# Routed experts in two halves: the down product in three float32r passes, run amid the next expert's gate and up products

## The chip, the cores and the metric

The kernel runs on one core of one Trainium2 chip. The metric is the device time of one execution in microseconds; the time of a version is the median of its runs.

## The reference, cut to what matters

Two transformer layers run one after the other on 512 tokens of width 1024. The first one ends in a mixture of 64 experts, of which each token takes 8, plus one shared expert. Only the routed experts are touched here:

```python
def swiglu(x, wg, wu, wd):
    return (jax.nn.silu(x @ wg) * (x @ wu)) @ wd
...
    def expert_block(acc, blk):
        tok, wt, e = blk
        yb = swiglu(h_pad[tok], w_e_gate[e], w_e_up[e], w_e_down[e]) * wt[:, None]
        return acc.at[tok].add(yb), None
...
    return swiglu(h, w_sh_gate, w_sh_up, w_sh_down) + routed[:n]
...
    return x + g_ffn * y.reshape(b, s, d)
```

`wg` and `wu` are 1024 x 256, `wd` is 256 x 1024, all float32. A block holds up to 128 tokens of one expert; with 512 tokens, 8 experts each and 64 experts, a block has 64 real tokens on the average and the rest of its 128 places is padding. `wt` is a token's weight for the expert and `g_ffn` a vector of 1024 gains.

## The kernel before

The stages follow one another: the first layer's mixing part (`block1`), the experts (`moe`), the second layer's mixing part (`mixer`) and its key-value lookup (`peer`). The experts take the stretch from about 620 to 1375 us of the profiled execution.

`moe` (line 764) loops over the 64 experts. Each has three weight loads of 1 MB on the SP queue (`expert_load`, line 1020; parts 0 and 1 hold gate and up, part 2 holds down) into nine rotating buffers called `raw`, and a gather of its token rows from `h2d` on the POOL queue (`next_rows`, line 1034) into one of three buffers `xg`. A 65th block (`spare`, line 1088, called at e = 32) takes tokens past the 128th of one expert; `overflow` (line 1092) is a loop for still more of them.

`expert_block` (line 1039) does one block:

- eight transposes of `xg` on TensorE and a split of the result into a high and a low float32r part `xt` (`split`, line 104: ScalarE copies to the high part, VectorE subtracts for the low part).
- gate and up product into one PSUM tile `p_gu`: the weights are split in four pieces of 128 x 1024 into pairs `whi`, `wlo` (three buffers of each, pool `pair`), and each piece feeds two chunks of three passes (`mm`, line 91: high by high, high by low, low by high). That makes 24 matmuls of 512 columns.
- `ea` = silu(gate) on ScalarE, times up on VectorE (lines 1060 and 1061), two transposes into `p_at`, a VectorE copy to `eat` (line 1066).
- the down product in plain float32 straight from the `raw` buffer (line 1072): two column halves by two chunks, four matmuls, which the profile shows as eight records.
- VectorE multiplies each half by the token weight and by `grow`, which holds g_ffn in every row (line 1075), and an indirect DMA on the POOL queue adds the 128 rows to one of two DRAM sums `yd` (line 1076). The padding places carry the row numbers 512 to 639, for which `yd` has 128 spare rows; the gather of line 1031 has the bound 511 and leaves out what lies past it.

Consecutive experts use the two sums in turn; experts 62 and 63 both add to `yd[1]`. While expert 63 runs, `routed_first` (line 1135) loads `yd[0]`, and `routed_second` (line 1144) adds it to the residual rows `xr`; `routed` (line 1200) does the same with `yd[1]` after the stage, and from there everything depends on it.

The order on each engine comes from the framework, which plays a timeline through as it builds and lets ready work go ahead (`schedule_with_timeline_sim=True`); instructions of the experts before and after are thus already mixed on TensorE. VectorE's order is the written one in the block of expert 63, and VectorE, ScalarE and SP follow the written order in `routed`.

Between the experts stands other work: `slots` every eighth (line 908, indices for the next eight experts, VectorE above all), `ffn_input` at e = 11, the shared expert in float32 (`shared`, `shared_down`) at eight of the experts, `by_tokens` at two.

## Time and profile before

| what | us |
|---|---|
| median of 3 runs | 3178.13 (3173.89 to 3178.19) |
| the profiled execution | 3173.92 |
| its span | 3172.1 |
| TensorE busy in the span | 3062.8 |
| VectorE / ScalarE / GpSimd busy | 2238.7 / 1383.4 / 578.9 |

The span is the time from the first to the last instruction of the profiled execution; 1.8 us of its own time lie around it. A matmul's duration runs from its start to its modelled end; since matmuls are pipelined, what one costs in a row of them is the distance between two starts. PE is TensorE's matmul row, PEld its weight loads, DVE VectorE, ACT ScalarE, POOL GpSimd, SP the engine that issues most DMAs.

### The profile page before, as it was taken

How to read it: one execution, taken by the hardware profiler on the slowest of the kernel's cores; microseconds unless marked ns; L12 is line 12 of the kernel's file. 1: busy time of each engine (PE TensorE's matmuls, PEld its weight loads, DVE VectorE, ACT ScalarE, POOL GpSimd, SP SyncE). 2: the span in 40 equal slices, each digit the busy share in tenths (PEclk: the TensorE clock that was granted, in tenths of full speed). 3: DMA queues.
4: the chain of work that ended last, by engine and by line, in shares of the span. 5: the costliest groups of instructions: out<-in, count | busy, mean ns of one | idle time of the engine just before them, and what ended most of it. 6: DMA issues, size and time to landing. Idle time of an engine off the chain costs nothing.

```text
span 3172.1 us, 43671 instructions
## 1 busy us (share of the span) xinstructions
PE 3062.8 (97%) x16232; PEld 2479.5 (78%) x16232; DVE 2238.7 (71%) x4079; ACT 1383.4 (44%) x2199; POOL 578.9 (18%) x448
## 2 busy tenths in 40 slices
PE   8999999999999999969999999999999999999999
PEld 4777888666666766657777788899999998888887
DVE  7467654587777777756633334899998887888887
ACT  5257423454444544434445324544444443333332
POOL 0200000122222222200000000033333233222221
PEclk9999999899999999989999999999999999999999
DMA  7554545399999999952121122487789989999997
GB/s 248 175 159 145 220 158 203 125 359 338 335 344 334 358 349 346 317 170 83 41 85 62 70 93 95 139 283 268 278 312 348 332 332 344 349 348 354 353 339 270
DMA packets 237626, 782.01 MB, mean 247 GB/s; under 512 B 28884, under 2 KB 110292, under 8 KB 191588
## 3 DMA queue, kind: packets, MB, share of 16 engines
q1 hardware_dynamic: 169072, 574.02, 49.0%
q0 software_dynamic: 65424, 198.81, 20.2%
q10 hardware_dynamic: 2916, 6.37, 0.6%
q8 instruction: 128, 2.10, 0.3%
q14 instruction: 86, 0.70, 0.1%
HBM read 694.38 MB, written 101.97 MB: 251 GB/s over the span
## 4 chain that ended last, share of the span: by engine, by line
PE 49%; DVE 6%; issue 1%; ACT 1%; DMA 1%; ACTq 0%; DVEq 0%; POOL 0%; POOLq 0%
PE p_y L102 16%; PE p_pu L102 12%; PE p_za L102 3%; PE p_z L102 2%; PE p_all L1267 2%; PE p_rg L102 1%; DVE wlo L106 1%; PE p_pq L102 1%; PE p_mx L102 1%; PE p_yr L102 1%; DVE prow L2010 1%; PE r_s L1614 1%; PE r_y L1624 1%; PE p_ya L102 1%; PE p_gt L1979 1%
## 5 line engine op out<-in xcount | busy, mean ns | idle before, releaser
L105 ACT ACTIVATE whi<-raw 128x1024 fp32r<-128x1024 f32 (+1 forms) x686 | 711.5, 1049 | 1135.4 <-PE p_pu L102 259.7
L106 DVE TENSOR_TENSOR wlo<-raw,whi 128x1024 fp32r<-128x1024 f32 (+1 forms) x686 | 822.6, 1207 | 350.2 <-ACT whi L105 338.9
L102 PE MATMUL p_pu<-xp,whi 128*128 128x384 f32 x2048 | 531.3, 338 | 5.0 <-ACT pact L1845 4.8
L102 PEld LDWEIGHTS p_pu<-xp,whi 128*128 128x128 f32 x2048 | 369.2, 188 | 7.9 <-ACT pact L1845 7.6
L102 PE MATMUL p_gu<-whi,xt 128*128 128x512 f32 x1040 | 356.8, 411 | 0.2 <-ACT whi L105 0.2
L102 PE MATMUL p_pu<-xp,wlo 128*128 128x384 f32 x1024 | 344.8, 338 | 4.7 <-DVE wlo L106 4.7
L102 PE MATMUL p_y<-whi,vhi 128*128 128x512 f32 x768 | 299.1, 389 | 3.0 <-ACT vhi L2060 1.6
L102 PE MATMUL p_y<-wlo,vhi 128*128 128x512 f32 x768 | 298.9, 389 | 0.0
L2000 POOL DMA_INDIRECT prow<-in_pu_rows,rows x128 | 198.0, 1547 | 513.9 <-DVE prow L2010 365.6
L1072 PE MATMUL p_y<-raw,eat 128*128 128x512 f32 x520 | 237.1, 597 | 2.7 <-DVE eat L1066 1.5
L102 PE MATMUL p_y<-whi,vlo 128*128 128x512 f32 x768 | 237.8, 389 | 0.0
L102 PEld LDWEIGHTS p_gu<-whi,xt 128*128 128x128 f32 x1040 | 197.4, 190 | 50.4 <-issue 11.2
L102 PE MATMUL p_gu<-wlo,xt 128*128 128x512 f32 x520 | 223.0, 429 | 4.9 <-DVE wlo L106 4.7
L2000 POOL DMA_INDIRECT prow<-in_pv_rows,rows x128 | 139.5, 1090 | 363.0 <-DVE yr L2016 349.7
L102 PEld LDWEIGHTS p_pu<-xp,wlo 128*128 128x128 f32 x1024 | 192.3, 188 | 10.4 <-DVE wlo L106 10.2
L1072 PEld LDWEIGHTS p_y<-raw,eat 128*128 128x128 f32 x520 | 97.7, 191 | 101.6 <-issue 89.5
L102 PEld LDWEIGHTS p_y<-whi,vhi 128*128 128x128 f32 x768 | 144.1, 188 | 33.5 <-ACT vhi L2060 2.0
L1076 POOL DMA_INDIRECT yd<-ey,gidx x64 | 117.5, 1836 | 285.1 <-DVE ey L1075 268.1
L102 PEld LDWEIGHTS p_y<-wlo,vhi 128*128 128x128 f32 x768 | 144.2, 188 | 30.0
L102 PEld LDWEIGHTS p_y<-whi,vlo 128*128 128x128 f32 x768 | 144.2, 188 | 29.9
L2016 DVE SCALAR_TENSOR_TENSOR yr<-prow,pdots,yr 128x1024 f32<-128x1024 f32 x128 | 163.8, 1280 | 0.2
L2010 DVE SCALAR_TENSOR_TENSOR prow<-prow,xr 128x1024 f32<-128x1024 f32 x128 | 155.5, 1219 | 3.1 <-DMA prow<-in_pu_rows,rows 3.0
(703 smaller groups left out, 5558.7 us busy)
## 6 DMA issues: line engine op xcount, KB each, us to landing
raw<-in_w_moe SPq DMA_DIRECT2D x195, 1024.0 KB
raw<-in_pu SPq DMA_DIRECT2D x64, 1024.0 KB
raw<-in_pv_rows SPq DMA_DIRECT2D x64, 1024.0 KB
raw<-in_w_mod SPq DMA_DIRECT2D x24, 1024.0 KB
gd<-gst SPq DMA_DIRECT2D x12, 2048.0 KB
vgt<-gd SPq DMA_DIRECT2D x32, 768.0 KB
actd<-pact SPq DMA_DIRECT2D x54, 384.0 KB
vact<-actd SPq DMA_DIRECT2D x54, 384.0 KB
```

Source lines behind the costliest of these rows:

```text
L102: nc.tensor.matmul(out, a, b, start=start and i == 0, stop=stop and i == len(passes) - 1)
L105: self.nc.scalar.activation(hi, src, AF.Copy)
L106: (lo_engine or self.nc.vector).tensor_tensor(lo, src, hi.bitcast(F32), ALU.subtract)
L1072: nc.tensor.matmul(py, at[:, 128 * k:128 * k + 128], wd[:, 1024 * k + 512 * n:1024 * k + 512 * n + 512], start=k == 0, stop=k == 1)
L1076: nc.gpsimd.indirect_dma_start(out=yd[:], out_offset=bass.IndirectOffsetOnAxis(ap=gi, axis=0), in_=y[:], in_offset=None, bounds_check=639, ...
L1267: self.nc.tensor.matmul(pts[i][:, :264], w[a][:, 128 * k:128 * k + 128], self.hn[b][:, k, 264 * i:264 * i + 264], start=k == 0 and n == 0, ...
L1614: nc.tensor.matmul(pt[:m, :n], self.rk[r:r + 64, g, 128 * kt:128 * kt + m], self.rq[r:r + 64, g, 512 - n:], start=True, stop=True)
L1624: nc.tensor.matmul(o, sts[kt][:, 128 * (i - kt):128 * (i - kt) + 128], v[:, 128 * kt:128 * kt + 128], start=False, stop=kt == i)
L1979: nc.tensor.matmul(pt[:, i, :], hots["hot2"][:, g, :, t], hots["ghi"][:, g, :, t], start=True, stop=False)
L2000: nc.gpsimd.indirect_dma_start(out=t[:], out_offset=None, in_=A["pu_rows" if i < 128 else "pv_rows"], in_offset=bass.IndirectOffsetOnAxis( ...
L2010: nc.vector.scalar_tensor_tensor(t, t, 1.0, self.xr, ALU.mult, ALU.mult, accum_out=dots[:, k:k + 1])
L2016: nc.vector.scalar_tensor_tensor(self.yr, t, dots[:, k:k + 1], self.yr, ALU.mult, ALU.add)
```

## The change

Five things are done. `expert_block` is cut into `expert_in` (transposes and split of the rows), `expert_up` (gate, up, and the product `ea`) and `expert_down` (the rest), and the loop runs the down half of expert e - 1 and the input half of expert e + 1 between the four pieces of expert e's gate and up product. The down product takes three float32r passes on split weights, two pieces more per expert through the `pair` buffers. The token weight goes into the product `ea`; VectorE's two evictions of the down product become ScalarE copies, and g_ffn is multiplied on the sums, in `routed_second` and `routed`. The scatter has the bound 511 and leaves out the padding places, so `yd` has 512 rows. `grow` lives in another pool.

```diff
-            self.yd = [d.tile([640, 1024], F32, name=f"yd{i}") for i in range(2)]
+            self.yd = [d.tile([512, 1024], F32, name=f"yd{i}") for i in range(2)]
...
+            down, xt = iter(()), self.expert_in(xg.pop(0))
+
+            def beside(down, e):
+
+                nonlocal xt
+                next(down, None)
+                yield
+                if e < 64:
+                    xt = self.expert_in(xg.pop(e))
+                yield
+                yield from down
+
             for e in range(64):
...
                     w[e] = self.expert_load(e)
-                    xg[e] = self.next_rows(self.gidx[:, e:e + 1])
+                if 2 <= e + 1 < 64:
+                    xg[e + 1] = self.next_rows(self.gidx[:, e + 1:e + 2])
...
-                    self.expert_block(xg.pop(e), self.gidx[:, e:e + 1], self.wsl[:, e:e + 1], w.pop(e), yd)
+                    other = beside(down, e + 1)
+                    up = self.expert_up(xt, self.wsl[:, e:e + 1], w.pop(e), other)
+                    for step in other:
+                        pass
+                    down = self.expert_down(*up, self.gidx[:, e:e + 1], yd)
                     if e == 63:
+                        for step in down:
+                            pass
                         self.routed_second()
...
                     self.mm(pg, (xt[0][:, k, :], xt[1][:, k, :]), (hi[:, 512 * kk:512 * kk + 512], lo[:, 512 * kk:512 * kk + 512]),
                             k == 0, k == 7)
+                next(other, None)
         a = ms.tile([128, 256], F32, name="ea", tag="ea")
         nc.scalar.activation(a, pg[:, :256], AF.Silu)
-        nc.vector.tensor_mul(a, a, pg[:, 256:])
+        nc.vector.scalar_tensor_tensor(a, a, ws, pg[:, 256:], ALU.mult, ALU.mult)
+        return a, part
+
+    def expert_down(self, a, part, gi, yd):
...
-        at = ms.tile([128, 256], F32, name="eat", tag="eat")
-        nc.vector.tensor_copy(at, pt[:, :256])
+        at = [ms.tile([128, 256], F32R, name=f"eat{i}", tag=f"eat{i}") for i in range(2)]
+        self.split(*at, pt[:, :256])
+        yield
         y = ms.tile([128, 1024], F32, name="ey", tag="ey")
         wd = part(2)
+        py = [ps.tile([128, 512], F32, name="p_y", tag="y") for n in range(2)]
+        for k in range(2):
+            hi, lo = (self.pair.tile([128, 1024], F32R, name=n, tag=n) for n in ("whi", "wlo"))
+            self.split(hi, lo, wd[:, 1024 * k:1024 * k + 1024])
+            for n in range(2):
+                self.mm(py[n], tuple(t[:, 128 * k:128 * k + 128] for t in at), (hi[:, 512 * n:512 * n + 512], lo[:, 512 * n:512 * n + 512]),
+                        k == 0, k == 1)
         for n in range(2):
-            py = ps.tile([128, 512], F32, name="p_y", tag="y")
-            for k in range(2):
-                nc.tensor.matmul(py, at[:, 128 * k:128 * k + 128], wd[:, 1024 * k + 512 * n:1024 * k + 512 * n + 512],
-                                 start=k == 0, stop=k == 1)
-            o = slice(512 * n, 512 * n + 512)
-            nc.vector.scalar_tensor_tensor(y[:, o], py, ws, self.grow[:, o], ALU.mult, ALU.mult)
+            nc.scalar.activation(y[:, 512 * n:512 * n + 512], py[n], AF.Copy)
         nc.gpsimd.indirect_dma_start(out=yd[:], out_offset=bass.IndirectOffsetOnAxis(ap=gi, axis=0),
-                                     in_=y[:], in_offset=None, bounds_check=639, oob_is_err=True, compute_op=ALU.add)
+                                     in_=y[:], in_offset=None, bounds_check=511, oob_is_err=False, compute_op=ALU.add)
...
     def routed_second(self):
         for x, y in zip(self.xr, self.y0):
+            self.nc.vector.tensor_mul(y, y, self.grow[:, None, :].to_broadcast([128, 2, 1024]))
             self.nc.vector.tensor_add(x, x, y)
...
         for t in range(4):
+            nc.vector.tensor_mul(ys[t], ys[t], self.grow)
             nc.vector.tensor_add(x[t], x[t], ys[t])
```

## Rows read from the trace of the kernel before

**Rows 1.** The page's busy time and share of the span, TensorE.
```profile
PE 3062.8 (97%) x16232; PEld 2479.5 (78%) x16232; DVE 2238.7 (71%) x4079; ACT 1383.4 (44%) x2199; POOL 578.9 (18%) x448
```

**Rows 2.** Windows: stretch, length, busy per engine (instructions), clock, DMA share, GB/s.
```profile
620.00:1358.00 738.00, 726.35 (x3110) 493.14 (x3107) 556.29 (x815) 358.28 (x479) 200.69 (x127) 0.99 0.97 335
...
740.00:780.00 40.00, 37.08 (x139) 23.64 (x137) 25.99 (x41) 19.55 (x28) 7.75 (x6) 0.91 0.87 305
```

**Rows 3.** Waits in 620 to 1358: total us, times, longest.
```profile
PE p_gu L102 <- DVE wlo L106: 4.7, 5, 1.6
...
DVE wlo L106 <- ACT whi L105: 90.2, 64, 7.1
...
ACT whi L105 <- PE p_gu L102: 239.4, 116, 10.2
```

**Rows 4.** DMA in 620 to 1358: queues (packets, MB, share), issues by line.
```profile
q1 hardware_dynamic: 27827, 197.42, 67.0%
q0 software_dynamic: 18144, 49.52, 29.9%
...
yd<-ey,gidx POOLq DMA_INDIRECT x63
xg<-h2d,gidx POOLq DMA_INDIRECT x62
```

**Rows 5.** Timeline of TensorE: start, us, one down product, then gate and up passes.
```profile
856.96 3.60 PE L1072 MATMUL p_y<-raw,eat 128*128 128x512 f32 x8
...
1328.21 0.39 PE L102 MATMUL p_gu<-wlo,xt 128*128 128x512 f32 x1
...
1330.30 0.40 PE L102 MATMUL p_gu<-wlo,xt 128*128 128x512 f32 x1
```

**Rows 6.** Groups of instructions in 620 to 1358: busy us, mean ns, idle before.
```profile
L106 DVE TENSOR_TENSOR wlo<-raw,whi 128x1024 fp32r<-128x1024 f32 x257 | 309.1, 1221 | 91.4 <-ACT whi L105 90.2
L105 ACT ACTIVATE whi<-raw 128x1024 fp32r<-128x1024 f32 x257 | 266.2, 1064 | 246.9 <-PE p_gu L102 239.4 <-PE p_at L1064 4.1 <-DVE ea L1061 0.9
L1072 PE MATMUL p_y<-raw,eat 128*128 128x512 f32 x520 | 237.1, 597 | 2.7 <-DVE eat L1066 1.5 <-DVE ey L1075 1.2
...
L1075 DVE SCALAR_TENSOR_TENSOR ey<-p_y,wsl,grow 128x512 f32<-128x512 f32 x128 | 91.3, 745 | 15.5 <-PE p_y L1072 15.2
L106 DVE TENSOR_TENSOR xt<-p_xt,xt 128x512 fp32r<-128x512 f32 x130 | 84.8, 684 | 15.8 <-ACT xt L105 15.7
...
L105 ACT ACTIVATE xt<-p_xt 128x512 fp32r<-128x512 f32 x130 | 71.7, 595 | 74.9 <-PE p_gu L102 65.8 <-PE p_xt L1046 7.6
...
L1066 DVE COPY eat<-p_at 128x256 f32<-128x256 f32 x65 | 27.4, 422 | 24.7 <-PE p_at L1064 24.0
L1061 DVE TENSOR_TENSOR ea<-ea,p_gu 128x256 f32<-128x256 f32 x65 | 26.8, 413 | 9.8 <-ACT ea L1060 9.8
L1060 ACT ACTIVATE ea<-p_gu 128x256 f32<-128x256 f32 x65 | 25.3, 390 | 26.2 <-PE p_gu L102 26.2
```

**Rows 7.** A window of the last layer in which VectorE is nearly full; columns as in Rows 2.
```profile
2220.00:2300.00 80.00, 75.59 (x422) 72.43 (x421) 78.61 (x291) 34.27 (x49) 29.83 (x18) 1.00 0.77 278
```

**Rows 8.** Timeline of the stage's end: start, us, engine, line.
```profile
1354.00 1.54 POOL L1076 DMA_INDIRECT yd<-ey,gidx  x1 [3.70 <-DVE ey L1075]
...
1357.85 0.75 DVE L1075 SCALAR_TENSOR_TENSOR ey<-p_y,wsl,grow 128x512 f32<-128x512 f32 x1 [0.96 <-PE p_y L1072]
...
1363.76 3.18 POOL L1076 DMA_INDIRECT yd<-ey,gidx  x1 [8.22 <-issue]
```

**Rows 9.** The chain that ended last, in order of time: start, us, what.
```profile
1363.76 10.65 DMA yd<-ey,gidx
```

**Rows 10.** Groups of VectorE instructions in 1358 to 1392; columns as in Rows 6.
```profile
L1217 DVE TENSOR_TENSOR h2f<-h2f,yx 128x1024 f32<-128x1024 f32 x4 | 4.9, 1217 | 0.0
L1146 DVE TENSOR_TENSOR h2f<-h2f,raw 128x2048 f32<-128x2048 f32 x2 | 4.6, 2286 | 4.6 <-DMA raw<-yd 4.6
```

More of the change, by code (lines that the diff above doesn't have):

```diff
@@ L347, in qkv @@
                         for y in self.yd:
-                            for i in range(5):
+                            for i in range(4):
                                 nc.gpsimd.dma_start(y[128 * i:128 * i + 128, :], self.macc)
@@ L716, in ffn_begin @@
         self.r4 = r.tile([128, 4], F32, name="r4")
+        self.grow = r.tile([128, 1024], F32, name="grow")
         r = self.pool(self.rs, "h2r", side="right")
@@ L771, in moe @@
             self.sact = q.tile([128, 2, 512], F32, name="sact")
-            self.grow = q.tile([128, 1024], F32, name="grow")
             self.xr = [t.rearrange("p a b -> p (a b)").rearrange("p (t d) -> p t d", d=1024) for t in self.h2f]
@@ L1039, in expert_block, with expert_in @@
     def expert_block(self, xg, gi, ws, w, yd):
+        for step in self.expert_down(*self.expert_up(self.expert_in(xg), ws, w), gi, yd):
+            pass
+    def expert_in(self, xg):
         nc, ps, ms = self.nc, self.mp, self.ms
@@ L1047, in expert_block, with expert_up @@
             self.split(*(t[:, 4 * g:4 * g + 4, :].rearrange("p a b -> p (a b)") for t in xt), pt)
+        return xt
+    def expert_up(self, xt, ws, w, other=iter(())):
+        nc, ps, ms = self.nc, self.mp, self.ms
         pg = ps.tile([128, 512], F32, name="p_gu", tag="mm")
@@ L1058, in expert_block @@
                             k == 0, k == 7)
+                next(other, None)
         a = ms.tile([128, 256], F32, name="ea", tag="ea")
         nc.scalar.activation(a, pg[:, :256], AF.Silu)
-        nc.vector.tensor_mul(a, a, pg[:, 256:])
+        nc.vector.scalar_tensor_tensor(a, a, ws, pg[:, 256:], ALU.mult, ALU.mult)
+        return a, part
+    def expert_down(self, a, part, gi, yd):
+        nc, ps, ms = self.nc, self.mp, self.ms
         pt = ps.tile([128, 512], F32, name="p_at", tag="tb")
```

## The prediction

> **What bounds the kernel now.** TensorE is busy in 97% of the span [rows 1], so I went to the windows of the one stage that the change touches, 620 to 1358 us: TensorE is busy in 726.35 of 738 us, VectorE in 556.29, ScalarE in 358.28, and the DMA engines in 97% of it [rows 2]. Two resources look full, and a reader has to decide which one sets the pace. The waits tell: what ScalarE waits for before it splits a weight piece is TensorE, 239.4 us in 116 times, because the `whi` buffers are still in use; VectorE waits 90.2 us for ScalarE; TensorE's matmuls wait for VectorE only 4.7 us [rows 3]. Nobody waits for a load worth speaking of. So TensorE sets the pace, its order being dense already, and every microsecond of its matmuls in this stage is a microsecond of the kernel. The DMA engines just keep up. That matters for the change: a stage that gets shorter with the same traffic would run into them.
>
> What fills them is uneven. The loads' queue takes 67.0% for 197.42 MB, that is 494 us or 2.50 us per MB; the POOL queue takes 29.9% (221 us) for 49.52 MB [rows 4]. The 63 scatters of 128 rows of 4 KB are 33.0 MB of this, and 16.5 MB are left for 62 gathers, 0.27 MB or 65 rows each. (The spare block's one of each is left aside.) So a gather whose bound is 511 does leave out the padding, and at the loads' price it needs 41 us; the scatters then take 180 us, 5.5 us per MB.
>
> **The change part by part.**
>
> *TensorE, the term that counts.* One down product today is eight records in 3.60 us, the last of them 0.597 long, so 0.429 from start to start and 3.43 us in all [rows 5, 6]. Nine gate and up passes lie between the starts 1328.21 and 1330.30, 0.232 each [rows 5] (the rows between, not shown, are such passes alone). Twelve passes of the same shape cost 2.79 us. The gain is 0.64 us per block, 42 us over 65 blocks, and TensorE's busy time goes from 726 to 684 us. Transposes stay as they are.
>
> The four float32 matmuls fit four passes of 0.215 us each. The Trainium skill, "FP8 and Floating Point Precision", TensorE Precision Notes, says that true FP32 takes four passes through the array; by that rule alone three passes would cost three quarters, which would save 0.86 us per block, 56 us. The rows give a float32r pass of this very shape 0.232, so I keep 42.
>
> *VectorE.* Added per block: two `wlo` subtractions of 1.221 us; the low part of `eat`, 128x256 out of PSUM, at 0.413 as the product `ea`, in place of the copy at 0.422; and the token weight in `ea`, between nothing and 0.061, the distance of the two 128x512 operations on PSUM at 0.745 and 0.684. I take the middle, 0.03. Removed: two evictions of 0.745 [rows 6]. That is +0.97 us, 63 us over 65 blocks: 556 becomes 619 us.
>
> *ScalarE.* Added per block: two `whi` copies of 1.064, the high part of `eat` (0.390, as the silu of the same shape), two evictions of 128x512 (0.595, as `xt`) [rows 6]: 3.71 us, 241 in all. 358 becomes 599 us. Neither engine reaches 684, but both come near, and the low part always waits for the high one.
>
> *How much TensorE will idle.* Nothing in the stage shows this load, so I bound it. Below: today's idle share, 11.65 of 738 us or 1.6%, at a VectorE share of 75% [rows 2]. Above: a stretch of the last layer with VectorE at 78.61 of 80 us (98%), where TensorE is idle 4.4 us, 5.5% [rows 7]. In a stage of 710 us VectorE has 87%, half way between, which gives 3.6%: 684 / 0.964 = 710 us. The stage gets 28 us shorter; with the lower bound 43, with the upper 14.
>
> *Moves.* Running a down product amid the next expert's pieces costs and saves TensorE nothing by itself, since its order is dense today; it keeps the longer chain (transposes, two splits, passes) off its path. If that cover goes, see the slower rival. The gather is issued one expert ahead by the program's order; POOL is busy 200.69 of 738 us [rows 2], and behind its scatter there waits only the next gather, whose rows have an expert's time. SP's loads wait for `raw` buffers; part 2 is now let go after its splits instead of after its matmuls, about as late. Of ScalarE's 246.9 us idle before `whi`, 244.4 are put down to engines and not to loads [rows 6]: taken as 0, at worst one load's 2.5 us [rows 4].
>
> *DMA.* With half the rows left out the scatters take 90 us instead of 180: engine time falls from 0.97 x 738 = 716 to 626 us, 88% of 710. This term gives nothing by itself, but without it the stage could not get below 716. Two of the ten zeroing DMAs of the sums, long before the stage, go as well: 0. The other pool of `grow`: 0.
>
> *The stage's end.* Today expert 63's last eviction ends at 1358.60, but its scatter starts only at 1363.76, since the one of expert 62, begun at 1354.00, adds to the same sum [rows 8]. In the new order 62's scatter starts before the last piece of 63's gate and up, some 7 us ahead of 63's last eviction: I take the wait of 5 us as gone. The last scatter needs 10.65 us to land [rows 9]; with half the rows between 5 less and the same, and I take the same. After it come four products with `grow` of the size of the 1.217 us additions, on VectorE, whose written order puts them on the path: +4.9 us. Two products of 128x2048 at 2.286 each [rows 10] fall while the last scatter lands: 0, or 4.6 if the cover is short. Sum 0, between -10 and +9.
>
> *Sum.* -28 + 0 us. The profiled execution took 3173.9, so 3146; it lies 4.2 us under the median of 3178.1, and the forecast against medians is **3150**.
>
> **The rivals.**
>
> *A, TensorE goes on setting the pace (the forecast):* -14 to -43 with the end's few us, 3135 to 3162. For it: TensorE has hardly a wait today [rows 3], and the new loads of the others stay under its own 684. Inside it, with 0.05: if a float32r pass cost only a quarter of a float32 matmul's 0.858 us, 0.215, the stage would lose 14 us more, 3136; the nine passes at 0.232 speak against it [rows 5]. It is the page's rule named above that would have it so.
>
> *B, ScalarE and VectorE in alternation:* their sums fit singly, but a low part needs its high part and a pair buffer, and both engines now also wait for TensorE more often (`eat`, evictions). If TensorE idles at least as much as in the stretch with VectorE full, 5.5%, the stage takes 684 / 0.945 = 724: -14, 3164, and with bursts (`slots`, `ffn_input`; in 740 to 780 TensorE had 37.08 of 40 us and a clock of 0.91 [rows 2]) up to 3178. Against it: six pieces per block spread evenly.
>
> *C, the padding isn't left out,* or an adding scatter pays for it all the same: the DMA engines need 716 us, the loads become the wait, and the stage saves 22 at most: 3156. The gathers speak against it [rows 4].
>
> *D, slower: ScalarE runs in order, and the down product's evictions stand before the next split.* While it waits for the last down pass, no pair is made; TensorE has then only the last piece's six passes, 6 x 0.232 = 1.39 us, and the next pair takes 1.064 + 1.221 = 2.28 us [rows 5, 6]. That is 0.89 us idle per block, 58 us over 65, against the 42 gained: +16, 3194. It decides as soon as the idle time per block passes 0.64 us. For it: only three pairs, six pieces per block, and evictions that were VectorE's. Against it: ScalarE keeps 16% of slack, and a build that plays the timeline through would put ready splits ahead of the evictions.
>
> **How the numbers follow.** A 0.57 with its own range 3135 to 3162, B 0.20, C 0.05, D 0.18. The range goes from 3128 (A with a scatter that lands sooner) to 3176 (most of B) and leaves out nearly all of D and little else. A measurement of this kernel can tell about 0.2% from no change, 6.4 us, so the borders are 3171.8 and 3184.5. Faster: A, C and 0.12 of B, 0.74. Same: 0.08 of B, 0.03 of D, 0.11. Slower: 0.15.
>
> **What would show it.** Right: p_y as 780 passes on `whi` and `wlo` about 0.232 apart; the stage some 28 us shorter, with TensorE's busy time near 684; VectorE's share 85 to 89%, ScalarE's 82 to 86%; the scatters' bytes halved and the DMA share under 0.92; the last scatter issued within a us of the last eviction; four products of 1.2 us before the additions behind it. B would show in TensorE's waits for `wlo` growing from 4.7 to some tens of us, C in 33 MB of scatters and ScalarE waiting for loads, D in a gap on TensorE in every block that a split ends, behind a ScalarE wait for the down product. The forecast is wrong if passes of the down product come further apart than 0.25, or if TensorE's idle share passes 5.5%.

## The result and the profile after

| | before | after |
|---|---|---|
| median of the runs, us | 3178.16 | 3213.7 (3211.17 to 3216.7) |
| ratio, 95% interval | 1 | 1.0118 (1.0106 to 1.013) |
| profiled execution / its span | 3173.92 / 3172.1 | 3212.86 / 3211.1 |
| first to last gate or up matmul of the stage | 729.0 | 762.2 |

The kernel became 1.2% slower, where 3150 was forecast. Of the 38.9 us that the span grew by, 33.2 lie between the first and the last gate or up matmul, 5.0 ahead of the stage and 0.8 behind it. In the runs below that share the changed kernel's code ahead of the stage, the stage begins anywhere between 619.7 us (e11) and 629.5 (e4), against 625.1 here and 620.1 before, so I leave these 5 us aside; their cause wasn't tried.

The windows of the stage, to the old end and to the new one; columns as in [rows 2]:

```profile
620.00:1358.00 738.00, 694.90 (x3288) 517.25 (x3287) 605.68 (x798) 543.31 (x771) 203.82 (x124) 0.99 0.90 310
620.00:1395.00 775.00, 723.20 (x3399) 536.86 (x3398) 630.05 (x825) 566.05 (x803) 210.11 (x128) 0.98 0.88 302
```

VectorE and ScalarE rose about as reckoned, to 82% and 74% of the first window. TensorE's busy time did not fall to 684: over the whole stage it is 723. The next views say why. First TensorE's timeline around a down product of the changed kernel:

```profile
685.22 0.63 PE L102 MATMUL p_y<-wlo,eat 128*128 128x512 f32 x2
686.06 0.50 PE L102 MATMUL p_gu<-whi,xt 128*128 128x512 f32 x1 [0.22 <-ACT whi L105]
686.40 0.87 PE L102 MATMUL p_y<-whi,eat 128*128 128x512 f32 x3
687.10 0.39 PE L102 MATMUL p_y<-wlo,eat 128*128 128x512 f32 x1
687.33 0.62 PE L102 MATMUL p_y<-whi,eat 128*128 128x512 f32 x2
...
691.36 0.50 PE L102 MATMUL p_gu<-wlo,xt 128*128 128x512 f32 x1 [0.16 <-DVE wlo L106]
```

Three passes from 686.40 to 687.10, one to 687.33: 0.23 apart, as forecast. But a pass behind a wait is recorded with 0.50 us in place of 0.39, and part of such a wait doesn't show as idle time. So stalls hide in the busy time, and here they are counted by starts. Each matmul is given its work: 0.232 us for a pass, 0.429 for a float32 record, 0.109 for a transpose, 0.033 for the few small ones. TensorE stalls where the next matmul starts later than the work of those before it would be done.

One thing has to be known for this count. The two rows behind the down product of [rows 5], which starts at 856.96:

```profile
859.99 0.80 PE L102 MATMUL p_gu<-wlo,xt 128*128 128x512 f32 x1
860.62 0.39 PE L102 MATMUL p_gu<-whi,xt 128*128 128x512 f32 x1
```

The pass behind the float32 records is recorded 3.03 us after their first start, only 0.03 after their last, but it is 0.80 long and the next one starts 0.63 after it. From 856.96 to 860.62 it is 3.66 us, which is eight records of 0.429 and one pass. So a down product did take 3.43 us, and the long pass behind it is no stall.

By this count the 729.0 us of the stage before are 701.4 of work and 27.6 of stalls, and the 762.2 after are 663.4 and 98.8. The work fell by 38 us (64 down products stand ahead of the last gate or up matmul now, 63 before), and the stalls grew by 71: +33. By the semaphore events, 51 of the 98.8 us end with a `whi` or a `wlo` of the weights, 6 of the 27.6 before. TensorE's idle share by its busy time, in the first window, is 5.8%, over the 5.5% that I had set as the mark of a wrong forecast; by starts it is 13% of the stage.

Who waits for whom, in 620 to 1395 us (total us, times, longest):

```profile
DVE wlo L106 <- ACT whi L105: 111.0, 124, 6.8
ACT whi L105 <- PE p_gu L102: 94.0, 80, 8.1
ACT whi L105 <- PE p_y L102: 77.7, 66, 8.1
...
PE p_gu L102 <- ACT whi L105: 20.3, 41, 1.1
...
PE p_gu L102 <- DVE wlo L106: 8.4, 24, 0.9
...
PE p_y L102 <- ACT eat L105: 3.9, 7, 1.2
```

Before, ScalarE waited for TensorE, and TensorE hardly for anybody [rows 3]. Now the waits go round: TensorE for ScalarE and VectorE, VectorE for ScalarE, ScalarE for TensorE, whose matmuls still hold the pair buffers. One expert's turn in the timeline of ScalarE and VectorE shows the round:

```profile
680.29 0.40 ACT L1090 ACTIVATE ea<-p_gu 128x256 f32<-128x256 f32 x1
680.56 2.98 ACT L105 ACTIVATE whi<-raw 128x1024 fp32r<-128x1024 f32 x3
...
683.56 0.39 ACT L105 ACTIVATE eat<-p_at 128x256 fp32r<-128x256 f32 x1
...
684.95 1.06 ACT L105 ACTIVATE whi<-raw 128x1024 fp32r<-128x1024 f32 x1 [1.00 <-PE p_gu L102]
...
687.07 1.06 ACT L105 ACTIVATE whi<-raw 128x1024 fp32r<-128x1024 f32 x1 [1.06 <-PE p_y L102]
...
688.04 1.07 ACT L1113 ACTIVATE ey<-p_y 128x512 f32<-128x512 f32 x2
688.16 1.23 DVE L106 TENSOR_TENSOR wlo<-raw,whi 128x1024 fp32r<-128x1024 f32 x1 [0.89 <-ACT whi L105]
...
688.99 1.06 ACT L105 ACTIVATE whi<-raw 128x1024 fp32r<-128x1024 f32 x1
...
689.94 1.09 ACT L105 ACTIVATE xt<-p_xt 128x512 fp32r<-128x512 f32 x2
690.08 1.23 DVE L106 TENSOR_TENSOR wlo<-raw,whi 128x1024 fp32r<-128x1024 f32 x1 [0.69 <-ACT whi L105]
...
690.89 0.40 ACT L1090 ACTIVATE ea<-p_gu 128x256 f32<-128x256 f32 x1
```

The turn takes 10.60 us (680.29 to 690.89). ScalarE splits three pieces at once, then has no free pair and waits 1.00 and 1.06 us for TensorE; VectorE waits 0.89 and 0.69 for ScalarE; TensorE, two rows of the first fence, waits for both. The window of the six turns from expert 2's `ea` to expert 8's, which hold no other work:

```profile
659.10:722.69 63.59, 61.34 (x278) 45.97 (x276) 54.04 (x61) 51.06 (x73) 20.88 (x13) 1.00 0.98 339
```

VectorE has 85% and ScalarE 80%, and TensorE's work is 9.44 us of a turn (36 passes, 10 transposes), 89%. No engine is full, each waits for another, and TensorE stalls 1.15 us a turn. ScalarE's order of this turn (three splits, `eat`, two splits, the evictions, one split, `xt`, `ea`) returns in 39 of the 45 turns between the second `ea` and the 47th.

The groups of instructions in the stage; columns as in [rows 6]:

```profile
L106 DVE TENSOR_TENSOR wlo<-raw,whi 128x1024 fp32r<-128x1024 f32 x387 | 463.3, 1223 | 112.6 <-ACT whi L105 111.0
L105 ACT ACTIVATE whi<-raw 128x1024 fp32r<-128x1024 f32 x387 | 399.0, 1068 | 172.6 <-PE p_gu L102 94.0 <-PE p_y L102 77.7
...
L1113 ACT ACTIVATE ey<-p_y 128x512 f32<-128x512 f32 x128 | 68.4, 586 | 0.1
...
L1091 DVE SCALAR_TENSOR_TENSOR ea<-ea,wsl,p_gu 128x256 f32<-128x256 f32 x64 | 30.3, 473 | 1.7 <-ACT ea L1090 1.7
```

387 pieces in place of 257, at the durations of before. In front of the evictions `ey` ScalarE waits 0.1 us in all. The DMA queues (packets, MB, share of 16 engines):

```profile
q1 hardware_dynamic: 28429, 200.27, 69.8%
q0 software_dynamic: 18497, 33.36, 18.1%
```

The scatters lost 16 MB [rows 4]: the padding is left out. The timeline of the stage's end, and then a row of the chain that ended last (start us, us, what):

```profile
1387.32 1.54 POOL L1114 DMA_INDIRECT yd<-ey,gidx  x1 [8.65 <-ACT ey L1113]
...
1390.77 0.15 DVE L1190 COPY raw<-raw 128x1 f32<-128x1 f32 x1 [4.60 <-DMA raw<-yd]
1390.84 0.47 DVE L1091 SCALAR_TENSOR_TENSOR ea<-ea,wsl,p_gu 128x256 f32<-128x256 f32 x1
...
1397.62 1.09 ACT L1113 ACTIVATE ey<-p_y 128x512 f32<-128x512 f32 x2 [5.15 <-PE p_y L102]
...
1398.98 2.15 POOL L1114 DMA_INDIRECT yd<-ey,gidx  x1 [10.12 <-ACTq L1133]
```

```profile
1398.98 6.79 DMA yd<-ey,gidx
```

The last scatter starts 0.27 us after the last eviction ends (1397.62 + 1.09 = 1398.71) and lands in 6.79 us, where before it started 5 late and took 10.65 [rows 8, 9].

### The profile page after: what moved, and what is told of

Same layout as the page of the kernel before. It is cut to its first block, busy times and chain, and to the rows that moved or that the text cites. A ratio compares the mean times of both kernels' runs of the same rounds, so it can differ in the third digit from the quotient of the medians.

```text
span 3211.1 us, 44724 instructions
## 1 busy us (share of the span) xinstructions
PE 3061.9 (95%) x16492; PEld 2523.0 (79%) x16492; DVE 2317.4 (72%) x4085; ACT 1591.9 (50%) x2524; POOL 588.2 (18%) x446
## 4 chain that ended last, share of the span: by engine, by line
PE 48%; DVE 6%; issue 1%; ACT 1%; DMA 1%; DVEq 0%; POOL 0%; POOLq 0%; ACTq 0%
PE p_y L102 16%; PE p_pu L102 11%; PE p_za L102 3%; PE p_z L102 2%; PE p_all L1307 1%; PE p_rg L102 1%; PE p_pq L102 1%; PE p_mx L102 1%; DVE wlo L106 1%; PE p_yr L102 1%; DVE prow L2050 1%; PE r_s L1654 1%; PE p_ya L102 1%; PE r_y L1664 1%; PE p_gt L2019 1%
## 5 line engine op out<-in xcount | busy, mean ns | idle before, releaser
L105 ACT ACTIVATE whi<-raw 128x1024 fp32r<-128x1024 f32 (+1 forms) x816 | 844.4, 1053 | 1053.1 <-PE p_pu L102 267.2
L106 DVE TENSOR_TENSOR wlo<-raw,whi 128x1024 fp32r<-128x1024 f32 (+1 forms) x816 | 977.0, 1210 | 375.9 <-ACT whi L105 366.3
L102 PE MATMUL p_gu<-whi,xt 128*128 128x512 f32 x1040 | 363.8, 409 | 22.6 <-ACT whi L105 20.3
L102 PE MATMUL p_y<-whi,eat 128*128 128x512 f32 x520 | 174.4, 410 | 5.3 <-ACT eat L105 3.9
L1114 POOL DMA_INDIRECT yd<-ey,gidx x64 | 103.1, 1610 | 323.4 <-ACT ey L1113 280.6
L1050 POOL DMA_INDIRECT xg<-h2d,gidx x64 | 107.3, 1677 | 246.8 <-PE p_at L1099 172.6
```

The source lines that it names most:

```text
L102: nc.tensor.matmul(out, a, b, start=start and i == 0, stop=stop and i == len(passes) - 1)
L105: self.nc.scalar.activation(hi, src, AF.Copy)
L106: (lo_engine or self.nc.vector).tensor_tensor(lo, src, hi.bitcast(F32), ALU.subtract)
L1050: self.nc.gpsimd.indirect_dma_start(out=xg[:], out_offset=None, in_=self.h2d, in_offset=bass.IndirectOffsetOnAxis(ap=gi, axis=0), bounds_c ...
L1114: nc.gpsimd.indirect_dma_start(out=yd[:], out_offset=bass.IndirectOffsetOnAxis(ap=gi, axis=0), in_=y[:], in_offset=None, bounds_check=511, ...
```

## The experiments

All kernels are the changed one with one edit, but for the run on the scatter's bound alone, which is the kernel before with that one edit. "Stage" goes from the first to the last gate or up matmul; the next three columns are distances between the silus (`ea` on ScalarE) number 0 and 10, 10 and 47, 47 and 64 of the stage, in us (the spare block has one too, so number 47 is expert 46's). "Stalls" are TensorE's, counted by starts as above, in the stage and in the same three parts (the rest lies ahead of the first silu). They compare better than the distances: e1's first ten turns hold 91.9 us of work, those of after 97.4, since the parts don't begin at the same place of a turn. The first ten turns hold little other work; the middle 37 have five of the eight turns with the shared expert, both with `by_tokens`, the spare block and most `slots`.

| kernel | median us | ratio, 95% | stage | 0-10 | 10-47 | 47-64 | stalls: 0-10, 10-47, 47-64 |
|---|---|---|---|---|---|---|---|
| before (profiled) | | 1 | 729.0 | 100.3 | 436.4 | 183.2 | 27.6: 0.7, 22.4, 2.8 |
| after | 3213.7 | 1.0118 (1.0106-1.013) | 762.2 | 110.5 | 437.8 | 204.2 | 98.8: 13.2, 47.9, 35.6 |
| e1, no split of down weights | 3169.9 | 0.9979 (0.997-0.9989) | 719.1 | 92.5 | 423.5 | 193.4 | 55.8: 0.5, 33.7, 19.6 |
| e2, float32 down | 3179.0 | 1.0011 (1.0-1.0022) | 731.4 | 101.6 | 431.0 | 189.4 | 26.6: 1.5, 17.5, 5.8 |
| e3, evictions on VectorE | 3218.3 | 1.0131 (1.0107-1.0155) | 764.1 | 110.3 | 440.2 | 202.5 | 100.7: 13.5, 50.7, 33.0 |
| e4, not interleaved | 3303.6 | 1.0397 (1.0372-1.0421) | 857.5 | 128.2 | 498.8 | 219.6 | 194.2: 31.4, 109.3, 50.2 |
| e5, four pairs | 3195.6 | 1.0073 (1.0056-1.0089) | 741.0 | 106.2 | 429.4 | 196.3 | 77.7: 8.6, 42.5, 25.1 |
| e6, five pairs | 3198.2 | 1.0072 (1.0055-1.0088) | 748.6 | 100.9 | 445.0 | 193.9 | 85.4: 5.8, 55.7, 22.6 |
| e7, three pairs, one `raw` less | 3196.6 | 1.0077 (1.006-1.0094) | 748.3 | 110.5 | 440.4 | 188.5 | 85.1: 13.2, 50.8, 19.5 |
| e8, before, bound 511 | 3176.3 | 1.0001 (0.999-1.0012) | 731.0 | 100.3 | 437.1 | 183.7 | 29.6: 0.6, 23.0, 3.3 |
| e9, no low parts | 3220.1 | 1.014 (1.0119-1.0161) | 770.5 | 104.0 | 443.4 | 213.7 | 107.2: 6.8, 57.1, 41.5 |
| e10, no high parts | 3208.9 | 1.0118 (1.0093-1.0142) | 761.4 | 99.7 | 455.7 | 195.4 | 98.1: 2.6, 69.0, 23.5 |
| e11, low parts on GpSimd | 3409.7 | 1.0742 (1.0724-1.076) | 965.3 | 149.6 | 563.4 | 241.7 | 302.0: 53.8, 176.5, 68.6 |
| e12, the same, four pairs | 3329.8 | 1.0488 (1.0471-1.0506) | 877.0 | 125.2 | 505.1 | 238.1 | 213.8: 30.3, 115.5, 66.9 |
| e13, three passes in 20 turns | 3197.5 | 1.0069 (1.0044-1.0093) | 744.6 | 101.5 | 441.4 | 190.8 | 56.8: 1.4, 37.2, 15.0 |
| e14, in the other 44 | 3196.3 | 1.007 (1.0048-1.0091) | 754.2 | 110.6 | 438.5 | 194.9 | 77.9: 13.3, 43.6, 18.5 |
| e15, splits written ahead | 3210.4 | 1.0107 (1.0083-1.013) | 760.0 | 110.4 | 437.8 | 202.7 | 96.6: 13.1, 47.8, 33.9 |
| e16, and kept in that order | 3216.0 | 1.0124 (1.0097-1.0151) | 767.7 | 112.1 | 448.0 | 195.2 | 104.4: 16.9, 58.5, 25.1 |
| e17, one of two pieces split | 3222.8 | 1.0155 (1.0132-1.0178) | 772.6 | 101.0 | 456.1 | 206.2 | 109.3: 3.9, 69.6, 34.0 |
| e18, one chunk split, one float32 | 3192.2 | 1.0061 (1.0038-1.0084) | 743.2 | 102.0 | 435.5 | 197.0 | 59.1: 1.7, 37.2, 19.2 |

**Which part of the change.** e1: the down passes run on `xt` in place of split weights.

```diff
-            self.split(hi, lo, wd[:, 1024 * k:1024 * k + 1024])
+        hi, lo = (t.rearrange("p a b -> p (a b)") for t in self.xt_of)
```

> The kernel after, but the down product's twelve passes run on the split token rows xt (same shape and type) in place of the split down weights, so its two pieces per block are not split and take no pair buffer; this leaves out the product with the real down weights. Theory S (the two extra pieces per block: six pieces now go through three pair buffers, ScalarE, VectorE and TensorE take turns, and TensorE waits for splits): the waits vanish and the passes' gain stands alone, 3145 to 3165 us, under the kernel before. Rival E (evictions on ScalarE hold up the splits): still over 3195. Rival O (the written order with the halves mixed is at fault): still over 3195. Rival P (three passes cost as much as float32): 3178 to 3190.

e2: float32 down as before, all else as after.

```diff
-        self.split(*at, pt[:, :256])
+        nc.vector.tensor_copy(at, pt[:, :256])
...
+                nc.tensor.matmul(py, at[:, 128 * k:128 * k + 128], wd[:, 1024 * k + 512 * n:1024 * k + 512 * n + 512],
```

> The kernel after with the down product back in plain float32 from the raw buffer (eat copied by VectorE, no pieces), everything else as after: halves mixed, evictions on ScalarE, token weight in ea, g_ffn on the sums, padding left out. Theory S: TensorE's waits for splits go back to the few of before, 3172 to 3188 us. Rival E: evictions still on ScalarE, over 3195. Rival O: over 3195. If it comes out under 3172, the other parts of the change gain by themselves.

e3: `nc.scalar.activation(y, py, AF.Copy)` becomes `nc.vector.tensor_copy(y, py)`.

> The kernel after with the two evictions of the down product as VectorE copies instead of ScalarE copies. Rival E: ScalarE is free to split, under 3190 us. Theory S: the pieces and buffers are the same, VectorE gets 1.3 us more per block: 3205 to 3240.

e4: each expert's down half runs out before the next expert begins.

```diff
-                    down = self.expert_down(*up, self.gidx[:, e:e + 1], yd)
+                    for step in self.expert_down(*up, self.gidx[:, e:e + 1], yd):
+                        pass
```

> The kernel after, but each expert's down half is written right after its own gate and up half instead of amid the next expert's; only the framework's own reordering mixes them. Rival O: under 3195 us. Theory S: the same six pieces per block through three buffers, 3205 to 3240.

e8: in the kernel before, `bounds_check=639, oob_is_err=True` becomes `bounds_check=511, oob_is_err=False`.

> The kernel before with one edit: the scatter has the bound 511 and leaves out the padding places. If the DMA engines do not set the pace of the kernel before: 3165 to 3180 us, no change or a few us from the shorter last scatter, with the scatters' bytes halved and the DMA share of the stage under 0.9. If they do: under 3140.

Measured: without the splits 3169.9, with float32 down 3179.0, level with the kernel before (e2's interval just reaches 1.0). So everything but the three-pass down product is neutral together: e2's stalls are those of before. The three-pass form brings 72 us of stalls over e2's and saves 41 of work. Without its two pieces per expert 43 of these stalls are gone, and the kernel gains 0.1 to 0.3%. It stays short of theory S (3145 to 3165), because 28 us more of stalls are left than before. They come after the first ten turns, where the built order alternates short and long turns (6.7 and 15.4 us, for instance), so e1 is no cap on what free splits could give. Evictions on VectorE change nothing for the better. The interleaving written by hand is worth 90 us to the three-pass form; that is outside both ranges of e4. And e8's queue carries the scatters without their padding, 32.91 MB in place of 49.52 [rows 4], at an unchanged time:

```profile
q0 software_dynamic: 18144, 32.91, 18.8%
...
620.00:1358.00 738.00, 726.06 (x3113) 493.39 (x3112) 555.43 (x813) 358.90 (x479) 200.66 (x127) 0.99 0.90 313
```

The DMA share fell from 0.97 to 0.90 and nothing followed: the DMA engines did not set the pace of the kernel before.

**Which engine, which buffer.** e9 takes the two `wlo` subtractions away (both operands are `hi`), e10 the two `whi` copies (`lo` is a subtraction from `grow`). e5 and e6 give `whi` and `wlo` a fourth and a fifth buffer for the stage, paid for with one and two of the nine `raw` buffers; e7 is the control of e5, three pairs and eight `raw`; e6 has none. In e9 and e10 the down pieces also leave the `wlo` or the `whi` buffers alone, so an engine's work and the use of its buffers go together there.

```diff
-            hi, lo = (self.pair.tile([128, 1024], F32R, name=n, tag=n) for n in ("whi", "wlo"))
+            pp = self.next_pair()
+            hi, lo = (pp.tile([128, 1024], F32R, name=n, tag=n) for n in ("whi", "wlo"))
```

> The kernel after without the low part of the down weights: ScalarE still makes the two high pieces per block, VectorE subtracts nothing for them, and the high piece stands in for the low one in the passes; this leaves out that part of the product. Pair buffers: the high ones are used as in the kernel after, the low ones only by gate and up. Theory V (VectorE's two subtractions, 2.4 us per block, make the others late): most of the loss goes, 3170 to 3185 us. Theory C (ScalarE's two copies and the high buffers that they take): under 10 us less than the kernel after, 3200 to 3215. If both share it: 3186 to 3199.

> The kernel after without the high part of the down weights: ScalarE makes no down piece, VectorE still does two operations of the subtraction's shape per block (raw minus grow) into the low buffers, and all passes run on these; this leaves out the real down product. Theory C: 3170 to 3185 us. Theory V: 3200 to 3215. Both: 3186 to 3199.

> The kernel after with a fourth pair buffer for the experts' pieces (used in rotation with the three), paid for with one of the nine weight buffers raw (RAW2 = 5). Theory S1 (what is short is the number of pair buffers: ScalarE waits for a free one, and TensorE starves behind it): the stage loses most of its 33 us, 3180 to 3198. Rival S2 (the buffers suffice; ScalarE and VectorE in turn, with the work that each has besides, cannot deliver six pieces per block in time): 3205 to 3220. Rival L (with a raw buffer less the loads come late): over 3220, with ScalarE waiting for loads.

> As the run before with five pair buffers and seven raw buffers (RAW2 = 4). S1: 3165 to 3190 us. S2: 3205 to 3220. L: over 3220, more than with four pairs.

> The kernel after with eight raw buffers instead of nine and three pairs as it has: the control of the two runs with more pairs. S1 and S2: 3208 to 3222 us, as the kernel after. L: over 3225.

In the first ten turns the answers are orderly. TensorE's stalls there with no, one and two pieces split: 0.5 us (e1), 3.9 and 1.7 (e17, e18, below), 13.2. With three, four and five pairs: 13.2, 8.6, 5.8. With either engine relieved of its two operations: 6.8 and 2.6. So neither engine alone is at its end; the round between them and TensorE over three pairs is what costs, some 1.2 us a plain turn for two pieces and 0.3 or less for one. The six plain turns of e10:

```profile
656.78:713.54 56.76, 56.76 (x278) 46.83 (x277) 54.02 (x61) 40.57 (x62) 21.74 (x13) 1.00 0.99 362
```

VectorE is busier here than in the changed kernel, 95%, and TensorE doesn't idle. The loads are the same, so they aren't what makes the changed kernel's turn 10.6 us long. The waits of e6 in its first ten turns, where the changed kernel has 13.1, 11.3 and 12.4 us for the same three:

```profile
DVE wlo L106 <- ACT whi L105: 5.4, 9, 1.6
ACT whi L105 <- PE p_gu L102: 4.9, 5, 2.4
...
ACT whi L105 <- PE p_y L102: 0.9, 1, 0.9
```

Over the whole stage the answers are not orderly. e9 (3220.1) and e6 (3198.2) fall in none of their ranges, and e10's 3208.9 lies in theory V's, which the plain turns contradict. e9 and e10 do less and are no faster. e5's 3195.6 is in the range of theory S1, but its control e7, forecast level with after, takes 3196.6, so over the whole kernel the fourth pair gives nothing beyond what one `raw` buffer less gives. e7 does the same work as after, takes the same time for the first ten turns and nearly for the next 37, and then saves 15.7 us. Windows of the last turns, after and then e7:

```profile
1183.72:1388.00 204.28, 182.86 (x815) 134.64 (x813) 159.83 (x189) 145.70 (x202) 45.31 (x30) 0.98 0.82 276
```

```profile
1183.45:1372.00 188.55, 180.46 (x817) 134.57 (x815) 160.63 (x190) 143.60 (x201) 45.96 (x30) 0.99 0.87 299
```

Nearly the same busy times in 16 us less. The built order differs there. e7 keeps the order described above to the 53rd turn, while in after, from the 47th on, the evictions slip back from turn to turn: behind the third split, behind `xt` and into the next turn. With one load buffer less the builder's timeline ran differently, and another order came out. It gives back 16 of the 36 us of stalls in this part.

**Another engine for the low parts.** e11 and e12 give the down pieces' subtraction to GpSimd (`self.split(..., nc.gpsimd)`), with three and four pairs.

> The kernel after with the low parts of the down weights made by GpSimd instead of VectorE (GpSimd is busy 28% of the stage). Theory V: under 3200 us if a subtraction takes GpSimd less than 3 us; with more, the pair buffer is held so long that it is no better. Theory C: 3205 to 3225.

> As the run before, with four pair buffers and eight raw buffers. The run with four pairs alone left TensorE 31 us of waits for low parts and 8 us for high ones. Theory V: under 3180 us, and if the passes' gain comes through under 3170, below the kernel before. Theory C: 3190 to 3200, as with four pairs alone.

Much slower, and in none of their ranges. The timeline of e11, GpSimd and VectorE:

```profile
709.97 5.26 POOL L106 TENSOR_TENSOR wlo<-raw,whi 128x1024 fp32r<-128x1024 f32 x2
...
712.08 5.38 DVE L106 TENSOR_TENSOR wlo<-raw,whi 128x1024 fp32r<-128x1024 f32 x2 [2.62 <-ACT whi L105]
```

A subtraction of 1.22 us on VectorE is 2.63 on GpSimd, and VectorE's own two, begun at 712.08, end at 717.46: 2.2 us after GpSimd's end at 715.23, as if they had begun only then.

**Place and order.** e13 and e14 take the three-pass form by turn, `(e + 1) in BESIDE` or not, where BESIDE holds the ten turns with the shared expert's or the token transposes' work and the ten behind them. e15 writes each split two pieces ahead of its matmuls, e16 also holds VectorE and ScalarE to the written order within a turn:

```diff
+        up(0)
+        S.append(self.piece(W[1], 0))
...
+            S.append(self.piece(W[1], 1))
+            down(0)
+            if plan:
+                nxt.append(self.piece(w[e + 1][0], 0))
+            down(1)
```

> Down product in three passes only in 20 of the 64 turns, those whose written place is at or just behind the shared expert's or the token transposes' work, where TensorE has work of its own that needs no splits; float32 down in the other 44 (everything else as in the changed kernel). Theory K (capacity: in a plain block VectorE and ScalarE have 9.6 us of work each, as seen in the changed kernel's windows, more than TensorE's 9.0 to 9.3, so three passes lose there and gain only beside TensorE's other work): 3170 to 3181, at or a little under the kernel with float32 down everywhere (3179). Theory O (only the built order of the queues is at fault, whichever block): no better than the share of three-pass blocks would give, 3179 + 20/64 of 35 = 3190, within 8.

> The complement: three passes in the 44 plain turns, float32 in the 20 beside other work. Theory K: 44 times 0.5 to 0.75 us over the kernel with float32 down (periods of 10.6 against 9.85 to 10.1 us), 3201 to 3212. Theory O: 3179 + 44/64 of 35 = 3203, within 8; the pair of runs tells the two apart, not this one alone: under K this one carries the whole loss.

> All down products in three passes, but each split is written two pieces ahead of its matmuls (the next expert's first two pieces too, whose loads are written one expert earlier); the order on the engines is still the builder's. Theory O: plain blocks of 9.3 to 9.7 us instead of 10.6, stage about 715 to 730, median 3165 to 3180. Theory K: ScalarE and VectorE are still to be alternated and hold 9.6 us of work in a plain block, so 10.1 to 10.6 per block, median 3195 to 3215.

> As the run with the splits written ahead, and VectorE and ScalarE keep that written order inside a turn (the same order in every block, no irregular later blocks). Theory O: the stage loses the irregular late blocks (some 15 us against the changed kernel) and the stalls of the plain ones, median 3160 to 3180. Theory K: plain blocks of 9.8 to 10.4 us, since two engines with 9.6 us of work each set the pace however they are ordered; without the irregular late blocks 3185 to 3200. If the mixing of other work (shared expert, slots) suffers from the fixed order, over 3215.

By place: in the first ten turns, all of them plain, e13 is at e2's time (101.5) and e14 at after's (110.6), so the loss there repeats. But e13 gains nothing where TensorE has other work: 441.4 and 190.8 against e2's 431.0 and 189.4. Theory K's half on that place falls, and both medians lie in theory O's ranges. (K's 9.6 us of work are sums of durations that overlap by 0.1 us each; the windows show VectorE with 95.94 and ScalarE with 86.09 of the first 110.54 us, and TensorE's work in a plain turn is 9.44, not 9.0 to 9.3. Capacity is not used up, and K falls in that form too.) By order: e15 is built into nearly the same order and time as after, 3210.4, where O had 3165 to 3180. e16 is regular to the end (195.2 against 204.2) and slower in the other two parts, so theory O, that the order alone is at fault, falls as well, as far as this order can tell. TensorE's order was still the builder's, and ScalarE waited for it:

```profile
696.50 0.39 ACT L105 ACTIVATE eat<-p_at 128x256 fp32r<-128x256 f32 x1 [2.01 <-PE p_at L1112]
```

**One piece.** e17 splits the first down piece and uses it for both chunks; e18 runs one chunk in three passes and the other in float32.

```diff
+        self.split(hi, lo, wd[:, :1024])
+        for n in range(2):
+            self.mm(py[n], tuple(at), (hi[:, 512 * n:512 * n + 512], lo[:, 512 * n:512 * n + 512]), True, False)
+            nc.tensor.matmul(py[n], a1, wd[:, 1024 + 512 * n:1536 + 512 * n], start=False, stop=True)
```

> All twelve passes of the down product, but only its first weight piece is split, and the passes of the second run on that pair too (the second piece's split is left out). ScalarE and VectorE have about 8.5 us of work each in a plain block, TensorE 9.0 to 9.1. Theory K with a threshold (a loss only where the two engines' work passes TensorE's): plain blocks of 9.1 to 9.5 us, stage 719 to 730, median 3168 to 3180, near the kernel without any split of the down weights (3170). A linear cost per split, wherever it falls: halfway between 3170 and 3214, 3188 to 3196, plain blocks of 9.8 to 9.9.

> The whole computation: of the down product's two chunks the first in three passes on a split piece, the second in plain float32 from the raw buffer. ScalarE and VectorE 8.4 to 8.5 us of work in a plain block; TensorE some 0.2 us under the kernel with float32 down. Threshold: plain blocks of 9.6 to 9.8 us, median 3165 to 3179, under the kernel before or level with it. Linear: 0.22 us saved against half of 0.75 lost per block, 3185 to 3195.

In the plain turns the cost is not linear: over the same six turns TensorE stalls 0.02 us a turn with e18's one piece, 0.33 with e17's and 1.15 with both. e18's turn of 9.78 us is the one that theory K's threshold forecast. Its 3192.2 is inside the linear range all the same, by luck: the loss is in the later turns (37.2 and 19.2 us of stalls against e2's 17.5 and 5.8), where the built order is irregular. e17's 3222.8 is in neither range: its first ten turns are near e18's, and the rest is 30 us slower than e18's with less work on TensorE. No complete version ran faster than the kernel before.

## Why the prediction was wrong

**What bounds the kernel: right.** TensorE set the pace (96% of the stage before is its work by starts), and e8 shows that the DMA engines did not.

**TensorE's term: right.** A float32 down product took 3.43 us before, and three passes take 2.78 (12 at 0.232): 0.65 per block, 42 us over 65 blocks. The work between the first and the last gate or up matmul fell by 38, as one more down product lies in there now. The rule that I weighed, four passes for true FP32 (the Trainium skill, "FP8 and Floating Point Precision", TensorE Precision Notes), would give a quarter off; the trace has 19% off, so the rule's quarter doesn't hold for the time here.

**VectorE's and ScalarE's terms: right.** Their windows to 1395 us hold 630 and 566 us, forecast 619 and 599. The product `ea` with the token weight takes 473 ns, where I had 443.

**How much TensorE will idle: the step that failed.** I took 3.6% from between two stretches by VectorE's share. The share came out near the forecast (82% over the first window, 87% in the first ten turns), and yet the stalls by starts grew by 71 us where the step allowed some 14. The share of one engine doesn't say what a round of three engines over three buffers costs: in the plain turns TensorE doesn't idle at a VectorE share of 95% (e10) and stalls 1.15 us of 10.6 at 85% (after). And the idle time that I read it from leaves out the stalls that hide in busy time: before it was 27.6 us of 729, 3.8%, not 1.6%. It is rival B's mechanism, ScalarE and VectorE in alternation, at a price that I capped far too low (724 to 738 for the stage). B's sign, TensorE's waits for `wlo` at some tens of us, came out at 8.4; its waits for `whi` went to 20.3, and most of the rest hides in the busy time.

In the first ten turns the runs show it: the stalls grew by 12 us over e2's, and they go with the number of pieces, with either engine's work and with the number of pairs. In the middle 37 turns they grew by 30; the round is the same and costs the same there (47.9 us, 1.3 a turn, as in the first ten), but no run shows it by taking something away: the versions that do are built in other orders there, and their stalls, 34 us (e1) to 70 (e17), don't follow the split work. What sets those **stays open**. In the last seventeen turns the stalls grew by 30, and e7 shows that with the work unchanged another built order gives 16 of these back. Whether some order of all three engines would win the 42 us was not tried.

**Moves: wrong in one thing.** I held that running the down half amid the next expert's pieces costs and saves nothing. The three-pass form needs it: e4 is 90 us slower than after.

**DMA: right.** The padding is left out, the share is 0.90 where 0.88 was forecast, and that gives nothing by itself (e8). That the stage could not get below 716 us without it was not tried.

**The stage's end: right to 3 us.** The wait of 5 us is gone, four products of 1.217 us are on the path, and the landing is 3.9 us shorter, inside the bounds. (In e8, the kernel before with the bound alone, the last scatter takes 9.19 us to land, so the bound isn't shown to give all of it.) From the last gate or up matmul to the next stage's first transposes it was 35.7 us before and is 32.8. One new wait was not forecast: in expert 63's written order a copy that waits for the load of `yd[0]` now stands ahead of `ea` on VectorE, which so begins 2.6 us after its silu's end (1387.88 + 0.38); the timeline of the stage's end above has both rows.

**The rivals.** C falls by the scatters' bytes. D's time (3194) was nearer than mine, but its mechanism is not the cause: ScalarE waits 0.1 us in front of the evictions, and moving them to VectorE (e3) brings nothing back. The slipping evictions of the last turns are a sign of that, not its cause: e3, where they are VectorE's, takes 202.5 us there.

## What to carry to other kernels

Where an engine must hand pieces to a second and a third through a few buffers, price an extra piece by the round it has to make, not by the shares of the engines: here two pieces a turn, each 1.07 and 1.22 us on two engines with time to spare, cost 1.2 us of the path, one piece 0.3 or less, and two more buffers gave more than half of it back while the work was plain. Count TensorE's stalls from start to start, since the busy time of a modelled pipeline hides the short ones, and behind a float32 product go by the second start, not the first. And where a builder's timeline orders the queues, a control that changes only a buffer count shows how much of a difference is order: here 16 us, more than half of the 28 that the change was to gain.

## What the runs showed of the hardware

A float32 matmul of 512 columns cost 0.858 us in a row (3.43 for four), a float32r pass 0.232, so three passes save 19%, not 25%. The pass behind a float32 product is recorded 0.03 us after the product's last record and 0.80 us long; the time shows in the start after it.

VectorE and GpSimd did not run two-input subtractions side by side in e11: VectorE's waited out GpSimd's 5.26 us. The Trainium skill, "SBUF — State Buffer", SBUF: two separate sides, has it that VectorE and GpSimd share a pair of ports as an exclusive lock, which an operation with two SBUF inputs takes for its whole length; the rows of e11 agree that VectorE waits, here through two of GpSimd's instructions.

The last scatter, with its padding left out, landed in 6.79 us in the changed kernel and in 9.19 in e8; with all 128 rows it took 10.65.
